# A decoder block on one core: triangular inverses from blocks of 32, their scratch on the weights' queue, and a diagonal by sums

## The chip, the cores and the metric

One core of a Trainium2 chip runs the whole program. The engines named below are TensorE (PE in the rows, its weight loads PEld), VectorE (DVE), ScalarE (ACT), GpSimd (POOL) and SyncE (SP, which here only issues transfers). The metric is the device time of one execution in microseconds. The matrices are float32; a large product is computed from two rounded parts (float32r) of each factor in three products.

## The reference, cut to what matters

One layer of a decoder on 256 positions of width 2048: a combined projection, three branches (gated delta rule with 8 heads, gated linear recurrence with 8 heads, attention into 256 memory tokens), their gated sum, an output projection and an MLP of width 8192. The change touches the first two branches:

```python
    lower = jnp.where(strict, bc[..., :, None] * jnp.einsum('bhnid,bhnjd->bhnij', kc, kc) * dec, 0.0)
    a_mat = lower + jnp.eye(CHUNK, dtype=lower.dtype)
    rhs = jnp.concatenate([vc * bc[..., None], kc * (bc * jnp.exp(gam))[..., None]], axis=-1)
    sol = lax.linalg.triangular_solve(a_mat, rhs, left_side=True, lower=True, unit_diagonal=True)
...
        dec = jnp.exp(jnp.where(causal[:, :, None], b_i[..., :, None, :] - b_i[..., None, :, :], -jnp.inf))
        a_i = jnp.einsum('bhtd,bhjd,bhtjd->bhtj', q_i, k_i, dec)
        o = (q_i * jnp.exp(b_i)) @ state + a_i @ v_i
...
    merged = ga * (oa @ w_br_a[l]) + gb * (ob @ w_br_b[l]) + gc * (oc @ w_br_c[l])
    x = x + rmsnorm(merged @ w_out[l], g_post_mix[l])
    m = jnp.square(jax.nn.relu(h2 @ w_mlp_in[l])) @ w_mlp_out[l]
```

The kernel takes chunks of 128 positions instead of 64, so it needs, for each of 8 heads and 2 chunks, the inverse of a unit triangular 128x128 matrix (the first excerpt), and for the second branch a 128x128 matrix `a_i` whose diagonal is a plain sum over the 128 features, since the decay there is 1.

## The kernel before, in words

The main stream is a row of units. A unit is 16 (or 8) tiles of 128 rows of a weight matrix by 512 columns; two tiles are a group: one load of 512 KB by SP into `w` (4 buffers), a rounded copy `wh` on ScalarE (line 174), the remainder `wl` on VectorE (line 175; 4 buffers of each), and products on TensorE, in `unit` 12 of 512 columns (lines 206 to 208), in `unit_joined` 8 of 512 and 8 of 256 columns (lines 225 and 227).

All other work is background: Python generators in a list `bg`. After a group, `tick` adds `rate[0]` to a credit and `pump` takes that many steps, a step being what a generator issues up to its next `yield`. Rates are set by stage: R1 while the first branch's q, k, v, z are projected (64 ticks), R2 in the attention branch (48), R3 in the second branch's projections (64), R4 in the gates of the first branch (48). The framework's scheduler may put an instruction ahead of earlier ones of its engine when its operands are there sooner; `pin` (`keep_in_program_order`) forbids it to stand ahead of the instruction of its engine that the code issues just before.

`gen_a`, once per group of four heads, is the delta rule: decays `dec`, Gram products `kk`, the triangular matrices `U` (8 per head group, transposed), then their inverses. VectorE solves the blocks of 16 on the diagonal: POOL copies these blocks to a DRAM scratch `scr` (8 transfers) and reads them back so that each partition holds its block's coefficients, `Lb` (8 transfers). In `for c in range(BL - 2, -1, -1)` (lines 885, 886) one product and one sum per column follow each other. Then rounds join pairs of blocks of 16, 32 and 64: products `pw` (line 916) and `pzt` (line 921) and eight transposes back into `X` (line 929), all on TensorE; the last round has narrow products of its own (lines 905 and 910). A plain float32 product is two instructions in the rows.

`gen_b` is the second branch. Its diagonal is computed by eight products of 128x128 per head group of which the identity mask keeps the diagonal alone (line 1064, tile `ad`). `gen_start` prepares constants beside the first units; its TensorE work is `rb`, `gcol`, `pc` and `pl`.

## Time and profile before

| | us |
|---|---|
| median of 3 runs (lowest, highest) | 1806.01 (1805.75, 1806.58) |
| profiled execution, its own time | 1806.44 |
| profiled execution, first to last instruction | 1804.7 |
| TensorE busy | 1793.5 |
| weight loads of TensorE busy | 1532.6 |
| VectorE busy | 1127.0 |
| ScalarE busy | 905.6 |
| GpSimd busy | 44.5 |

Busy time is the union of an engine's instructions over the span. Instructions of TensorE overlap in the records, so a group's mean duration is longer than the time that one more of them takes; what a piece takes is read from the chain of waits, where pieces follow each other in time.

### The profile page before, as it was taken

Reading aid. Unit: us, or ns where it says so; the run is one execution under the profiler, and the core shown is the slowest. Engines: PE = TensorE matmul, PEld = TensorE weight load, DVE = VectorE, ACT = ScalarE, POOL = GpSimd, SP = SyncE. Lnnn points to the kernel's source line nnn. Section 1 sums busy time; section 2 is a strip of 40 time slices with the busy share of each in tenths; the row PEclk is TensorE's granted clock in tenths of the full one; section 3 lists DMA queues with packets and bytes.
Section 4 is the critical chain, followed back from the end, with each engine's and each line's share of the span. In section 5 each row is a group of like instructions: output and inputs, shape, how many; then the busy total and the mean of one; then the engine's idle time right before and its main releaser. Section 6 shows DMA issues by size and latency. Waiting matters only on the chain.

```text
span 1804.7 us, 23851 instructions
## 1 busy us (share of the span) xinstructions
PE 1793.5 (99%) x9241; PEld 1532.6 (85%) x9241; DVE 1127.0 (62%) x1518; ACT 905.6 (50%) x1156; POOL 44.5 (2%) x68
## 2 busy tenths in 40 slices
PE   9999999999999999999999999999999999999998
PEld 7888888888888888888888888888888888888886
DVE  5865678755764677696555557655655565655556
ACT  6645565544555565555444445544444444444433
POOL 1000000200200000000000000000000000000000
PEclk9999999999999999999999999999999999999999
DMA  8665645754665556465666674666666676666664
GB/s 264 207 194 160 185 146 168 209 172 138 177 187 152 158 169 187 141 186 175 198 186 187 213 232 152 191 193 191 195 186 198 188 220 187 195 187 195 188 194 139
DMA packets 174946, 333.40 MB, mean 185 GB/s; under 512 B 13144, under 2 KB 14832, under 8 KB 174576
## 3 DMA queue, kind: packets, MB, share of 16 engines
q1 hardware_dynamic: 169280, 325.10, 58.7%
q10 hardware_dynamic: 4528, 4.54, 0.9%
q0 software_dynamic: 1024, 2.23, 0.7%
q8 instruction: 72, 1.18, 0.3%
q14 instruction: 42, 0.34, 0.1%
HBM read 329.60 MB, written 2.23 MB: 184 GB/s over the span
## 4 chain that ended last, share of the span: by engine, by line
PE 97%; DVE 1%; DMA 1%; ACT 1%; issue 0%; SPq 0%; DVEq 0%; POOLq 0%; POOL 0%; ACTq 0%
PE mm L225 23%; PE mm L206 18%; PE mm L207 18%; PE mm L208 18%; PE mm L227 12%; PE pa L1120 1%; DMA w<-in_w_kv_mem 0%; PE pzt L921 0%; PE pw L916 0%; PE mm L373 0%; PE mm L375 0%; PE mm L372 0%; DVE wl L175 0%; DMA w<-in_w_in 0%; DVE cv L718 0%
## 5 line engine op out<-in xcount | busy, mean ns | idle before, releaser
L175 DVE TENSOR_TENSOR wl<-w,wh 128x1024 fp32r<-128x1024 f32 x600 | 728.5, 1223 | 540.2 <-ACT wh L174 456.3
L174 ACT CAST wh<-w 128x1024 fp32r<-128x1024 f32 x600 | 628.0, 1052 | 719.0 <-PE mm L208 453.7
L206 PE MATMUL mm<-wh,hh 128*128 128x512 f32 x576 | 227.5, 395 | 0.3 <-DVE sum L266 0.3
L208 PE MATMUL mm<-wh,hh 128*128 128x512 f32 x576 | 224.7, 390 | 0.0
L225 PE MATMUL mm<-h2h,wh 128*128 128x512 f32 x960 | 224.4, 390 | 0.0
L207 PE MATMUL mm<-wl,hh 128*128 128x512 f32 x576 | 224.4, 390 | 0.0
L225 PEld LDWEIGHTS mm<-h2h,wh 128*128 128x128 f32 x960 | 178.3, 188 | 35.8
L206 PE MATMUL mm<-wh,mh 128*128 128x512 f32 x512 | 199.2, 389 | 0.0
L207 PE MATMUL mm<-wl,mh 128*128 128x512 f32 x512 | 199.2, 389 | 0.0
L208 PE MATMUL mm<-wh,ml 128*128 128x512 f32 x512 | 199.2, 389 | 0.0
L225 PE MATMUL mm<-hh,wh 128*128 128x512 f32 x768 | 184.8, 391 | 0.3 <-ACT z L730 0.3
L225 PEld LDWEIGHTS mm<-hh,wh 128*128 128x128 f32 x768 | 141.0, 188 | 27.8 <-ACT z L730 0.5
L208 PEld LDWEIGHTS mm<-wh,hh 128*128 128x128 f32 x576 | 108.1, 188 | 22.7
L206 PEld LDWEIGHTS mm<-wh,hh 128*128 128x128 f32 x576 | 108.2, 188 | 21.8 <-DVE sum L266 0.5
L207 PEld LDWEIGHTS mm<-wl,hh 128*128 128x128 f32 x576 | 108.3, 188 | 21.1
L227 PEld LDWEIGHTS mm<-h2h,wl 128*128 128x128 f32 x960 | 119.3, 192 | 2.3
L227 PE MATMUL mm<-h2h,wl 128*128 128x256 f32 x960 | 120.3, 283 | 0.0
L207 PEld LDWEIGHTS mm<-wl,mh 128*128 128x128 f32 x512 | 96.1, 188 | 20.0
L208 PEld LDWEIGHTS mm<-wh,ml 128*128 128x128 f32 x512 | 96.1, 188 | 19.9
L206 PEld LDWEIGHTS mm<-wh,mh 128*128 128x128 f32 x512 | 96.1, 188 | 19.9
L227 PE MATMUL mm<-hh,wl 128*128 128x256 f32 x768 | 102.2, 284 | 0.0
L227 PEld LDWEIGHTS mm<-hh,wl 128*128 128x128 f32 x768 | 98.9, 191 | 3.4
(388 smaller groups left out, 1913.9 us busy)
## 6 DMA issues: line engine op xcount, KB each, us to landing
w<-in_w_in SPq DMA_DIRECT2D x240, 512.0 KB, 4.0
w<-in_w_mlp_in SPq DMA_DIRECT2D x128, 512.0 KB, 4.0
w<-in_w_mlp_out SPq DMA_DIRECT2D x128, 512.0 KB, 4.2
w<-in_w_out SPq DMA_DIRECT2D x32, 512.0 KB, 4.1
w<-in_w_kv_mem SPq DMA_DIRECT2D x30, 512.0 KB, 4.9
w<-in_w_br_c SPq DMA_DIRECT2D x16, 512.0 KB, 4.1
w<-in_w_br_a SPq DMA_DIRECT2D x16, 512.0 KB, 4.5
w<-in_w_br_b SPq DMA_DIRECT2D x16, 512.0 KB, 3.6
```

Of the source, the lines that this page charges most:

```text
L174: q(A.copy(wh[:, js, 0:width], w[:, js, 0:width]))
L175: q(V.tensor_tensor(out=wl[:, js, 0:width], in0=w[:, js, 0:width], in1=wh.bitcast(F32)[:, js, 0:width], op=ALU.subtract))
L206: T.matmul(o, st, wh[:, j, :], start=kt == 0, stop=False)
L207: T.matmul(o, st, wl[:, j, :], start=False, stop=False)
L208: T.matmul(o, sl, wh[:, j, :], start=False, stop=kt == nk - 1)
L225: T.matmul(ps[c], wh[:, j, c * P:(c + 1) * P], both[j], start=k0 + j == 0, stop=end)
L227: T.matmul(ps[c][:, 0:S], wl[:, j, c * P:(c + 1) * P], both[j][:, 0:S], start=False, stop=end)
L1120: T.matmul(pas[h][:, t * 192:t * 192 + 192], kp[:, h, t * P:(t + 1) * P], qp[:, h * 2 + t, 0:192], start=True, stop=True)
```

## The change

Five things, beside new rates. (1) The blocks solved by substitution are of 32: of each pair of blocks of 16 the second is solved as before, then the coefficients between the two (`Lx`) are multiplied with it and summed, the first block's coefficients are read from the scratch, and a second substitution solves it. The joining round of width 16 is not run. (2) The scratch's transfers are issued by SP: 12 writes and 16 reads, then 4 reads between the two substitutions, per head group. (3) After the round of width 32 only the quarter of `X` that the last round reads is transposed back, in eight transposes of 64x64. (4) The diagonal in `gen_b` is the sum over partitions of k times q, by products with ones, in two rounded parts. (5) The first instruction of each background step on VectorE, ScalarE and TensorE is pinned. Beside these, `dec` gets a yield between VectorE's and TensorE's part, and the four TensorE pieces of `gen_start` stand in one step.

```diff
-R1, R2, R3, R4 = 1.1, 1.0, 1.0, 1.2
+R1, R2, R3, R4 = 1.1, 1.2, 1.2, 1.27
...
-    V, A, T, G = nc.vector, nc.scalar, nc.tensor, nc.gpsimd
+    G = nc.gpsimd
+    pin = tc.keep_in_program_order
+    class Placed:
+        def __init__(self, engine):
+            self.engine, self.step_begins = engine, False
+        def __getattr__(self, name):
+            op = getattr(self.engine, name)
+            def issue(*args, **kwargs):
+                ins = op(*args, **kwargs)
+                if self.step_begins:
+                    pin(ins)
+                    self.step_begins = False
+                return ins
+            return issue
+    V, A, T = Placed(nc.vector), Placed(nc.scalar), Placed(nc.tensor)
+    def step_marks(begins):
+        for e in (V, A, T):
+            e.step_begins = begins
...
         while n > 0 and bg:
+            step_marks(True)
             try:
                 next(bg[0])
                 n -= 1
             except StopIteration:
                 bg.pop(0)
+            step_marks(False)
...
+        rrs = []
+        for t in range(NT):
+            rrs.append(g4("rr", (P, P)))
+            V.tensor_scalar(out=rrs[t], in0=ones, scalar1=rsm[:, t:t + 1], scalar2=None, op0=ALU.mult)
+        yield
+        pt = bank("cols")
+        pg, pc, pl = pt[:, 256:288], pt[:, 288:384], pt[:, 384:392]
+        for t in range(NT):
+            T.matmul(pt[:, t * P:(t + 1) * P], rrs[t], ident, start=True, stop=True)
+        T.transpose(pg, grow, ident[0:32, 0:32])
+        T.transpose(pc, crow, ident[0:96, 0:96])
+        T.transpose(pl, lrow, ident[0:8, 0:8])
...
             dl = g4("dl", (P, 2, 4, P), F32R)
-            pd = bank("dec")
             for i, l_ in enumerate((ldh, ldl)):
                 V.tensor_tensor(out=dl[:, i], in0=bc(caus, 4),
                                 in1=l_.bitcast(F32)[:, t, hs].unsqueeze(2).to_broadcast([P, 4, P]), op=ALU.mult)
+            yield
+            pd = bank("dec")
+            for i in range(2):
                 T.matmul(pd, mgtr, dl[:, i].rearrange("p h i -> p (h i)"), start=i == 0, stop=i == 1)
...
+        scr = dp.tile([NB // 2, 3, 8, BL, BL], F32, tag="scr", name=nm("scr"))
+        Lx = [g4("Lx", (P, 4, BL * BL)) for t in range(NT)]
+        def spread(rows, src):
+            nc.sync.dma_start(rows, src.rearrange("k b c m -> k (b c m)").to_broadcast([rows.shape[0], rows.shape[1]]))
         for k in range(NB):
-            sl = slice(k * BL, (k + 1) * BL)
-            pin(G.dma_start(scr[k].rearrange("b c m -> c b m"), U[sl, :, sl]))
+            sl, w = slice(k * BL, (k + 1) * BL), k % 2 * 2
+            nc.sync.dma_start(scr[k // 2, w].rearrange("b c m -> c b m"), U[sl, :, sl])
         for k in range(NB):
-            G.dma_start(Lb[k * BL:(k + 1) * BL].rearrange("p b m -> p (b m)"),
-                        scr[k:k + 1].rearrange("k b c m -> k (b c m)").to_broadcast([BL, 8 * BL * BL]))
+            spread(Lb[k * BL:(k + 1) * BL].rearrange("p b m -> p (b m)"), scr[k // 2, k % 2 * 2:k % 2 * 2 + 1])
+        yield
+        for k in range(NB // 2):
+            r0 = 2 * k * BL
+            nc.sync.dma_start(scr[k, 1].rearrange("b c m -> c b m"), U[r0:r0 + BL, :, r0 + BL:r0 + 2 * BL])
+        for k in range(NB // 2):
+            r0 = 2 * k * BL
+            for t in range(NT):
+                spread(Lx[t][r0:r0 + 2 * BL].rearrange("p b m -> p (b m)"), scr[k, 1:2, t * 4:t * 4 + 4])
         yield
...
+        def substitute(w):
+            pin(V.memset(Lb[:, :, 0:BL * BL:BL + 1], 1.0))
+            for c in range(BL - 2, -1, -1):
+                n = BL - c
+                tm = lp.tile([P, 8, BL], F32, tag="tm", name=nm("tm"), bufs=2)
+                V.tensor_tensor(out=tm[:, :, 0:n], in0=Xc[:, :, w, c:BL], in1=Lb[:, :, c * BL + c:(c + 1) * BL],
+                                op=ALU.mult)
+                V.tensor_reduce(out=Xc[:, :, w, c], in_=tm[:, :, 0:n], axis=AX.X, op=ALU.add)
+                if c % 2 == 0:
+                    yield
+        yield from substitute(1)
+        for k in range(NB // 2):
+            spread(Lb[(2 * k + 1) * BL:(2 * k + 2) * BL].rearrange("p b m -> p (b m)"), scr[k, 0:1])
+        V.tensor_scalar(out=Xc[:, :, 0, :], in0=Xc[:, :, 1, :], scalar1=rsecond, scalar2=None, op0=ALU.mult)
+        for t in range(NT):
+            ts = slice(t * 4, t * 4 + 4)
+            lx = Lx[t].rearrange("p b (c m) -> p b c m", c=BL)
+            V.tensor_tensor(out=lx, in0=Xc[:, ts, 0, :].unsqueeze(2).to_broadcast([P, 4, BL, BL]), in1=lx, op=ALU.mult)
+            yield
+            V.tensor_reduce(out=Xc[:, ts, 0, :], in_=lx, axis=AX.X, op=ALU.add)
+            yield
+        yield from substitute(0)
+        V.scalar_tensor_tensor(out=Xc[:, :, 0, :], in0=Xc[:, :, 1, :], scalar=rfirst, in1=Xc[:, :, 0, :],
+                               op0=ALU.mult, op1=ALU.add)
...
-        for s in (s_ for s_ in (2, 4, 8, 16, 32, 64) if s_ >= BL):
+        for s in (s_ for s_ in (2, 4, 8, 16, 32, 64) if s_ >= 2 * BL):
...
+            if s == 32:
+                pt = bank("X")
+                for b in range(8):
+                    T.transpose(pt[0:64, b * 64:(b + 1) * 64], XT[0:64, b, 0:64], ident[0:64, 0:64])
+                A.copy(X[0:64, :, 0:64], pt[0:64, :].rearrange("p (b i) -> p b i", b=8))
+                yield
+                continue
...
         AT = g4("AT", (P, 8, P))
-        for t in range(NT):
-            pd = bank("ad")
-            for h in range(4):
-                T.matmul(pd[:, h * P:(h + 1) * P], k[:, h, t * P:(t + 1) * P], q[:, h, t * P:(t + 1) * P],
-                         start=True, stop=True)
-            V.tensor_tensor(out=AT.rearrange("p (h t) i -> p h t i", t=NT)[:, :, t, :],
-                            in0=pd.rearrange("p (h i) -> p h i", h=4), in1=bc(ident, 4), op=ALU.mult)
+        kq, kqh, kql = g4("kq"), g4("kqdh", dt=F32R), g4("kqdl", dt=F32R)
+        V.tensor_tensor(out=kq, in0=k.rearrange("p h s -> p (h s)"), in1=q.rearrange("p h s -> p (h s)"), op=ALU.mult)
+        yield
+        A.copy(kqh, kq)
+        V.tensor_tensor(out=kql, in0=kq, in1=kqh.bitcast(F32), op=ALU.subtract)
+        yield
+        for hp in range(2):
+            pd, cs = bank("ad"), slice(hp * 512, hp * 512 + 512)
+            T.matmul(pd, onesr, kqh[:, cs], start=True, stop=False)
+            T.matmul(pd, onesr, kql[:, cs], start=False, stop=True)
+            V.tensor_tensor(out=AT[:, hp * 4:hp * 4 + 4, :], in0=pd.rearrange("p (b i) -> p b i", b=4), in1=bc(ident, 4),
+                            op=ALU.mult)
         yield
```

## Rows read from the trace of the kernel before

**Rows 1.** The page: busy time of the engines and the share of the span, the granted clock in 40 slices, and the chain that ended last by engine.
```profile
PE 1793.5 (99%) x9241; PEld 1532.6 (85%) x9241; DVE 1127.0 (62%) x1518; ACT 905.6 (50%) x1156; POOL 44.5 (2%) x68
...
PEclk9999999999999999999999999999999999999999
...
PE 97%; DVE 1%; DMA 1%; ACT 1%; issue 0%; SPq 0%; DVEq 0%; POOLq 0%; POOL 0%; ACTq 0%
```

**Rows 2.** Who TensorE waited for: us in total, times, the longest. These are all its waits.
```profile
PE idle L336 <- POOL ident L84: 1.6, 1, 1.6
PE mm L373 <- DVE memT L277: 0.4, 1, 0.4
PE mm L225 <- ACT z L730: 0.3, 1, 0.3
PE mm L206 <- DVE sum L266: 0.3, 1, 0.3
```

**Rows 3.** The chain of waits from 385 to 424 us, where the first head group's blocks are joined: start, us, what.
```profile
389.14 1.73 PE pw L916 x16
390.87 0.29 PE mm L206
...
393.69 1.73 PE pzt L921 x16
...
398.22 0.87 PE X L929 x8
...
414.58 1.07 PE pw L905 x16
415.65 0.43 PE mm L206
```

**Rows 4.** The same view from 546 to 582 us, the second head group's round of width 16.
```profile
547.75 1.73 PE pw L916 x16
549.48 1.97 PE mm L227 x16
```

**Rows 5.** The same view from 630 to 640 us, the first head group's diagonal.
```profile
633.35 1.79 PE ad L1064 x16
```

**Rows 6.** The same view from 272 to 284 us, the first head group's dec products.
```profile
275.90 0.47 PE dec L798
...
276.60 0.31 PE dec L798
...
279.67 0.23 PE dec L798
```

**Rows 7.** Groups of instructions of VectorE and, in the second row, of ScalarE: line, operation, tiles and shapes, count, then busy us, mean ns of one, and idle time before them with what ended most of it. The last row is of another view, VectorE's busy time from 327 to 375 us in the instructions that write or read the tile xc.
```profile
L175 DVE TENSOR_TENSOR wl<-w,wh 128x1024 fp32r<-128x1024 f32 x600 | 728.5, 1223 | 540.2 <-ACT wh L174 456.3
L174 ACT CAST wh<-w 128x1024 fp32r<-128x1024 f32 x600 | 628.0, 1052 | 719.0 <-PE mm L208 453.7
...
L744 DVE TENSOR_REDUCE ss<-sq 128x8 f32<-128x1024 f32 x4 | 4.9, 1218 | 4.0 <-ACT sq L742 4.0
L796 DVE TENSOR_TENSOR dl<-caus,ldl 128x512 fp32r<-128x512 f32 x4 | 2.7, 684 | 0.0
L889 DVE TENSOR_TENSOR X<-xc,mblk 128x1024 f32<-128x1024 f32 x2 | 2.4, 1222 | 0.0
...
327.00:375.00 48.00, 7.76 (x31) 1.00 0.76 207
```

**Rows 8.** The chain of waits from 33 to 40 us, the constants' TensorE work.
```profile
36.13 0.44 PE rb L491 x4
...
36.81 0.17 PE gcol L106
...
37.21 0.15 PE pl L507
37.37 0.43 PE mm L207
```

**Rows 9.** Who ScalarE waited for, in total us, times and the longest: the rounded copies of weights for TensorE (units of 12 products), and for the landing of w_in's weights.
```profile
ACT wh L174 <- PE mm L208: 453.7, 289, 4.3
...
ACT wh L174 <- DMA w<-in_w_in: 11.3, 6, 2.7
```

**Rows 10.** Transfers: the queues (packets, MB, share of 16 engines' span), KB and us to landing of the weights' and the scratch's transfers, how long the weights' issue takes on SP (ns, least, median, most), and what POOL waited for before issuing the reads (us, times).
```profile
q1 hardware_dynamic: 169280, 325.10, 58.7%
...
q0 software_dynamic: 1024, 2.23, 0.7%
...
w<-in_w_in SPq DMA_DIRECT2D x240, 512.0 KB, 4.0
...
scr<-U POOLq DMA_DIRECT2D x16, 8.0 KB, 3.4
...
L163 SPq DMA_DIRECT2D w<-in_w_in x240: 367/368/639, 90.3 to 968.8; - x120
...
  DMA scr<-U: 1.9, 3
```

**Rows 11.** VectorE in two stretches: us, its busy time and instructions, granted clock, mean busy share of the 16 DMA engines, GB/s. The first has the first head group's scratch transfers, the second its substitution.
```profile
330.00:350.00 20.00, 13.41 (x21) 1.00 0.95 228
350.00:385.00 35.00, 25.15 (x48) 1.00 0.66 197
```

**Rows 12.** Groups of TensorE's instructions, by form: the wide products of the joins of width 16 and 32 in both head groups; busy us, mean ns of one.
```profile
L916 PE MATMUL pw<-X,U 128*128 128x64 f32 x64 | 7.6, 271 | 0.0
```

More of the change, by code (lines that the diff above doesn't have):

```diff
@@ L89, in tile_trunk @@
     x_r = a["x"][0].rearrange("(t p) n -> p t n", p=P)
-    pin = tc.keep_in_program_order
     def adma(out, in_):
@@ L418, in gen_masks @@
         pin(V.tensor_copy(mgtr, mgt))
+        pin(V.tensor_copy(onesr, ones))
         pin(V.tensor_copy(msk2[:, 0, :], mlt))
@@ L426, in gen_masks @@
             if b < P:
-                cur = mblk if b == BL else cst.tile([P, P], F32, tag=f"blk{b.bit_length() % 2}", name=f"blk{b}")
+                cur = cst.tile([P, P], F32, tag=f"blk{b.bit_length() % 2}", name=f"blk{b}")
                 v3 = cur.rearrange("p (n s) -> p n s", s=b)
@@ L438, in gen_masks @@
             pin(V.tensor_tensor(out=mT[s], in0=d, in1=mlt, op=ALU.mult))
+            if s == BL:
+                pin(V.tensor_tensor(out=mblk, in0=cur, in1=mT[s], op=ALU.subtract))
+                pin(V.tensor_reduce(out=rfirst, in_=mT[s], axis=AX.X, op=ALU.add))
+                pin(V.tensor_scalar(out=rfirst, in0=rfirst, scalar1=1.0 / BL, scalar2=None, op0=ALU.mult))
+                pin(V.tensor_scalar(out=rsecond, in0=rfirst, scalar1=-1.0, scalar2=1.0, op0=ALU.mult, op1=ALU.add))
             prev = cur
@@ L486, in gen_start @@
         yield
-        pb = bank("rb")
-        for t in range(NT):
-            rr = g4("rr", (P, P))
-            V.tensor_scalar(out=rr, in0=ones, scalar1=rsm[:, t:t + 1], scalar2=None, op0=ALU.mult)
-            T.matmul(pb[:, t * P:(t + 1) * P], rr, ident, start=True, stop=True)
-        V.tensor_copy(rbm, pb[:, 0:S])
-        yield
-        load_x()
-        turn_grow(grow, 32, 16)
-        yield
-        pc = bank("pc")
-        T.transpose(pc[:, 0:96], crow, ident[0:96, 0:96])
-        V.tensor_copy(ccol, pc[:, 0:96])
+        load_x()
+        yield
         for nm_, t in (("gn_a", gna), ("gn_b", gnb)):
@@ L505, in gen_start @@
         load_x()
-        pl = bank("pl")
-        T.transpose(pl[:, 0:8], lrow, ident[0:8, 0:8])
+        rrs = []
[10 more added lines that the diff above has]
+        T.transpose(pl, lrow, ident[0:8, 0:8])
+        V.tensor_copy(rbm, pt[:, 0:S])
+        V.tensor_copy(gcol[:, 16:48], pg)
+        V.tensor_copy(ccol, pc)
         raw, e, lb = small("raw", 8), small("e", 8), small("lb", 8)
@@ L877, in gen_a @@
         V.memset(W, 0.0)
-        V.memset(Lb[:, :, 0:BL * BL:BL + 1], 1.0)
-        Xc = lp.tile([P, 8, BL], F32, tag="xc", name=nm("xc"))
-        V.tensor_copy(Xc, dblk.unsqueeze(1).to_broadcast([P, 8, BL]))
+        Xc = lp.tile([P, 8, 2, BL], F32, tag="xc", name=nm("xc"))
+        V.tensor_copy(Xc[:, :, 1, :], dblk.unsqueeze(1).to_broadcast([P, 8, BL]))
         yield
-        for c in range(BL - 2, -1, -1):
-            n = BL - c
-            tm = lp.tile([P, 8, BL], F32, tag="tm", name=nm("tm"), bufs=2)
-            V.tensor_tensor(out=tm[:, :, 0:n], in0=Xc[:, :, c:BL], in1=Lb[:, :, c * BL + c:(c + 1) * BL], op=ALU.mult)
-            V.tensor_reduce(out=Xc[:, :, c], in_=tm[:, :, 0:n], axis=AX.X, op=ALU.add)
-            if c % 2 == 0:
-                yield
@@ new lines, in gen_a @@
+        yield from substitute(0)
+        V.scalar_tensor_tensor(out=Xc[:, :, 0, :], in0=Xc[:, :, 1, :], scalar=rfirst, in1=Xc[:, :, 0, :],
+                               op0=ALU.mult, op1=ALU.add)
+        V.tensor_tensor(out=X.rearrange("p b (k c) -> p b k c", c=2 * BL),
+                        in0=Xc.rearrange("p b w c -> p b (w c)").unsqueeze(2).to_broadcast([P, 8, NB // 2, 2 * BL]),
+                        in1=mblk.rearrange("p (k c) -> p k c", c=2 * BL).unsqueeze(1).to_broadcast([P, 8, NB // 2, 2 * BL]),
+                        op=ALU.mult)
@@ L1060, in gen_b @@
         AT = g4("AT", (P, 8, P))
[L1061 to L1067 removed]
+        kq, kqh, kql = g4("kq"), g4("kqdh", dt=F32R), g4("kqdl", dt=F32R)
[9 more added lines that the diff above has]
+            V.tensor_tensor(out=AT[:, hp * 4:hp * 4 + 4, :], in0=pd.rearrange("p (b i) -> p b i", b=4), in1=bc(ident, 4),
+                            op=ALU.mult)
         yield
```

7 lines of the change are left out of this document (2 added, 5 removed).

## The prediction

> **What bounds the kernel now.** I read the page first. TensorE is busy 99% of the span at a granted clock of 9 tenths or more in every slice (mean 0.999, the 2.4 GHz level throughout), and the chain of work that ended last lies on TensorE for 97% [rows 1]. The reader is to see that no other engine is near: VectorE 62%, ScalarE 50%. Busy is not yet bound, so the next view is who waits: TensorE waited 2.6 us in all, 1.6 of it at the very start [rows 2]. Then the chain in short stretches, because there the pieces follow one another without gaps and so give what each piece really takes: a 512-column product takes 0.23 us [rows 6], a 256-column one 1.97 / 16 = 0.12 [rows 4]. A background step (a block of other TensorE work between two weight groups) appears as one piece, and the product after it is a little longer. So the time is the sum of TensorE's pieces, and the question is which pieces the change takes out, and whether anything makes TensorE wait.
>
> That reading has a critic. The Trainium skill, page "Perfetto Trace Analysis", section "Identifying the Most-Contended Engine", says matmul occupancy is a bad measure of how near TensorE is to its limit and that the busy share of weight loads should be used. Here that share is 85% [rows 1], which by the rule leaves 15% of headroom; the pieces that follow each other without a gap do not agree. It is a rival below.
>
> **Taken out on TensorE.** Per head group (there are two):
> - The join round of width 16 goes. In the first group it is 1.73 (pw x16) + 1.73 (pzt x16) + 0.87 (X x8), and the product behind pw takes 0.29 instead of 0.23 [rows 3], which I take behind pzt too: 4.45 us. In the second group pw is 1.73 again [rows 4]; counted the same. Two groups: -8.9 us.
> - In the round of width 32 the eight transposes back (like the 0.87 of [rows 3]) become eight of 64x64. The nearest row is the 64x64 products: 16 in 1.07, and 0.20 more on the product behind [rows 3], so eight cost 0.54 + 0.20 = 0.74. Bounds: 0.74 to the old 0.87. I take 0.74: -0.3 us for both.
> - The diagonal of AT: sixteen pieces, 1.79 us [rows 5], become four 512-column products, 4 x 0.23 = 0.92. Two groups: -1.7 us. Its cover is gone if the operand (product, rounding, remainder, one step each) is late; the nearest row of a late operand is dec, where a product takes 0.47 instead of 0.23 [rows 6]. Bound: +0.24 per step, 0.5 in all.
> - The four dec products stand in the same step as the VectorE work they need and cost 0.47 + 0.31 + 0.23 + 0.23 = 1.24 (the fourth like the third) [rows 6]. With a yield between them they should cost 0.92: -0.6 us. Bounds 0 to -0.6; I take -0.6, since one step later is a whole weight group (12 x 0.23 = 2.7 us) and two of the VectorE products take 1.4 [rows 7].
> - At the start rb, gcol, pc and pl run as two blocks, with 0.43 on the product behind the second [rows 8]. As one block they save one such break: -0.2 us, bounds 0 and -0.4.
>
> Sum: -8.9 - 0.3 - 1.7 - 0.6 - 0.2 = -11.7 us.
>
> **Added on VectorE.** The second substitution repeats 30 small instructions: the 31 instructions on xc before the joins take 7.76 us, of which X takes 1.22 [rows 7], so 6.5. The two products over Lx and the two sums are 1024 wide, 1.22 each by the nearest rows [rows 7]: 4.9. A memset and two small ones of 6.5 / 30 = 0.22 each: 0.7. kq and its remainder add 2 x 1.22. Together 14.5 us per group, 29 us on an engine with 1804.7 - 1127.0 = 678 us idle: costed at nothing. What hides it: ScalarE waits for TensorE to give back the split-weight buffers (453.7 us in the units of 12 products alone [rows 9]), so the splits run ahead as far as four buffers allow. Three groups of 2.7 us less one rounding (1.05) and one remainder (1.22) [rows 7] leave about 5.9 us in which VectorE may be late. In the substitution itself (22 steps at 1.2 steps per group: 18.3 groups, 50 us) VectorE has 13.1 + 4.9 + 0.7 + 1.2 (X) = 19.9 us of steps and 18.3 x 1.22 = 22.3 of splits, 84%: it holds, with little to spare for evacuations. ScalarE loses four copies per group and gains two: nothing.
>
> **Moved to SP.** Per group POOL issued 8 writes and 8 reads; SP now issues 12 writes, 16 reads and later 4 more, at 0.37 us each by the weights' own row [rows 10]: 12 us in three bursts. SP is in order, so every weight load (one per 2.7 us) stands behind them, and the reads wait for the writes' landing (3.4 us median; POOL stood 1.9 us for it in all [rows 10]). The bytes: queue 0 took 0.7% of 16 engines' span for 2.23 MB, i.e. 202 us of engine time, 91 us per MB, against 52 for the weights [rows 10]. The first burst grows from 1.05 MB to 2.1 MB of reads: 2.1 x 91 / 16 = 12 us of all sixteen engines, 6.8 at the weights' rate. Against that, a weight load may be late by: four buffers x 2.7 = 10.9 between one split and the next in the same buffer, less 2.3 for the split, less 4.0 landing [rows 10] = 4.6 us until ScalarE waits, plus the 5.9 above = 10.5 until TensorE waits. In the old burst the engines were 95% busy [rows 11], ScalarE waited for weights 11.3 us over the whole w_in [rows 9], and TensorE not once [rows 2]. New lateness: between 0 (loads slip in between, as nothing pins the order) and 12 + 3.4 + 12 x 0.37 = 19.8 us. The two ends of the cost are 0 and 9.3 us per group. I take 0.3 per group, the near end: old lateness was absorbed with all of the 5.9 left, and twice that is still about the slack.
>
> The Trainium skill, page "DMA: Bandwidth & Descriptors", section "Queues, rings and completion order", says each engine consumes one ring's descriptors in order and takes turns between rings, which speaks against this move: before, weights took turns with the scratch, now they stand behind it. Its section "Issuing engines are not separate DMA queues" says the issuing engine only changes issue time. By the first the cost leans to the far end, by the second it is the extra bytes alone. No row here shows which holds for a burst on the weights' own queue.
>
> **Kept in place, and the rates.** A pin lets a step's first instruction start no earlier than its predecessor in the code. On TensorE there is little that runs early: gcol, pc and pl stand in one block though the code yields between them [rows 8]. What early or late steps cost TensorE is about 1 us (0.4 + 0.3 + 0.3 of waits after the start [rows 2], and the long dec pieces), part of it counted above. So the pins are costed at nothing, bounds -0.5 to +1. Steps: each group gains 2 (dec) + 1 (scratch) + 12 (sums, second substitution) - 3 (round) = 12, and gen_b 2, 28 in all; the rates give 48 x 0.2 + 64 x 0.2 + 48 x 0.07 = 25.8 more. So the background ends about where it did, two steps over; those stand beside the next unit, 22 us long.
>
> **The sum.** -11.7 + 0.6 (SP) = -11.1 on the profiled execution's span of 1804.7, 1806.44 in its own time; the median is 1806.01, 0.4 lower, and taking the change from it gives 1794.9 us.
>
> **The rivals.**
> - Weights partly late behind the scratch: 3 us per group, a third of the far end, 1806.0 - 11.7 + 6 = 1800.3. For: the engines' 95% and a queue in order. Against: 10.5 us of slack and no wait in the old burst.
> - VectorE cannot keep up in the substitution: 16% more work than reckoned, from evacuations and a late transfer back, fills the 50 us; 8 us more than that, less the slack of 5.9, is a wait of some 2 us per group, 1806.0 - 11.7 + 4 = 1798.3. For: the 84%. Against: in the old substitution VectorE was busy 25.15 of 35 us [rows 11] and TensorE did not wait.
> - Slower: every scratch transfer of a burst is issued ahead of the next weight load in both groups and served in order: 19.8 us late, 9.3 waited, twice: 1806.0 - 11.7 + 18.6 = 1812.9. It turns to slower where a load is late by more than 16.4 us (10.5 + 5.9) in each group.
> - TensorE is not the bound, something else fills the freed pieces: 1806. Against: its pieces leave no gap. For it stands only the 85%.
> - More than the sum: the pins also end the small waits after early steps and the dec and start pieces save their utmost, 1793.0.
>
> **How the numbers follow.** Forecast 0.71 (its own range 1793.3 to 1797.5), weights partly late 0.12, VectorE 0.06, slower 0.04, TensorE not the bound 0.02, more than the sum 0.05. What a measurement can tell from no change is about 0.2%, 3.6 us: faster is below 1802.4. The forecast, VectorE, more, and all but 0.02 of weights partly late are faster: 0.92. The 0.02 and the not-bound case are the same: 0.04. Slower 0.04. Range 1792.5 to 1801: outside it lie the slower and unbound cases, the upper end of the late weights and little below.
>
> **What would show it.** Right: the wide products of the joins (now 64 instructions at L916 [rows 12] and as many at L921) halve to 32 each, AT comes as four pieces of 0.23 us per group, the last TensorE piece ends some 11 us earlier and TensorE's waits stay under 4 us in all. Wrong: a wait of TensorE on DMA or on VectorE's wl near 330 or 500 us, ScalarE's wait for weights well above 11.3 us with pieces of 512 columns over 0.23 behind it, or products behind the steps that got longer everywhere.

## The result: slower, 1811.6 us

The changed kernel takes 1811.58 us (median of 12 runs, 1809.17 to 1815.41) beside 1806.55 for the kernel before in the same rounds (12 runs, 1805.75 to 1806.82): a ratio of 1.003, interval 1.0021 to 1.0039. The forecast was 1794.9. The profiled execution is the fastest of the 12 (1809.17 in its own time, span 1807.5), so what its trace shows of the loss is the least of it. Of the runs below, only the profiled one of e1, at a granted clock of 0.65 throughout, is left out of the numbers.

From the page of the changed kernel: busy times, to be laid beside [rows 1]. Its instructions on VectorE, ScalarE and TensorE all carry line 56 (the wrapper that pins), so they are read by their tiles.

```profile
PE 1787.8 (99%) x9137; PEld 1521.5 (84%) x9137; DVE 1153.0 (64%) x1599; ACT 904.6 (50%) x1150; POOL 25.5 (1%) x36
```

The page's chain gives TensorE 79% here, but its shares add up to 86% only, so they are not to be laid beside the 97% of [rows 1]; e10 below, which lost almost nothing, has 82%. The waits say more. Who TensorE waited for in the changed kernel (us in total, times, the longest), beside [rows 2]; below it a row of who ScalarE waited for, beside [rows 9]:

```profile
PE mm L56 <- ACT wh L56: 4.4, 3, 2.3
PE mm L56 <- DVE wl L56: 3.2, 6, 0.8
PE idle L56 <- POOL ident L109: 1.6, 1, 1.6
...
ACT wh L56 <- DMA w<-in_w_in: 22.5, 13, 5.3
```

TensorE waits 11.1 us in all instead of 2.6, nearly all of it more for the two parts of weights, and ScalarE waits twice as long for w_in's landing. The pieces that were to become shorter did. The changed kernel's chain of waits from 395 to 470 us, where the first head group's blocks are joined, beside [rows 3]:

```profile
425.62 1.73 PE pw L56 x16
...
430.17 1.73 PE pzt L56 x16
...
434.73 0.56 PE X L56 x8
...
438.23 1.07 PE pw L56 x16
```

One wide round instead of two, and the eight small transposes in 0.56 (0.87 before, [rows 3]). To sum this over the span I took for every background block the time from the product before it to the product behind it, less two usual products (0.227 each, 0.1196 for 256 columns): 117.8 us over all blocks before, 107.2 now, 10.6 less. The same sum over the main stream alone, its time beyond the usual products, is 3.9 us before and 17.3 now. Less 10.6 and plus 13.4 is the span's 2.8 more. The 13.4 stand in three places: 1.6 in the first 50 us, 7.6 at 330 to 365 us (by estimate 1.7 of them at TensorE's lower clock, see the last section), 3.5 at 505 to 570, and 0.7 elsewhere. The stretches of the scratch transfers, by windows (us, then busy time and count of PE, PEld, DVE, ACT, POOL, granted clock, DMA share, GB/s), first of the kernel before and then of the changed one:

```profile
330.00:365.00 35.00, 35.00 (x166) 29.28 (x165) 24.71 (x46) 19.66 (x33) 5.81 (x12) 1.00 0.82 213
505.00:570.00 65.00, 65.00 (x393) 57.81 (x392) 39.78 (x63) 34.62 (x42) 0.00 (x0) 1.00 0.56 166
```

```profile
330.00:365.00 35.00, 30.20 (x126) 23.59 (x125) 21.10 (x35) 15.05 (x20) 2.04 (x1) 0.95 0.82 210
505.00:570.00 65.00, 62.62 (x342) 53.86 (x342) 45.10 (x81) 36.35 (x52) 0.00 (x0) 1.00 0.77 202
```

What SP issued in the first of them, in the changed kernel (start us, us, what):

```profile
318.70 6.57 SPq L188 DMA_DIRECT2D w<-in_w_in  x3
330.93 3.65 SPq L893 DMA_DIRECT2D scr<-U  x8
334.63 3.66 SPq L889 DMA_DIRECT2D lb<-scr  x8
338.33 3.89 SPq L899 DMA_DIRECT2D scr<-U  x4
343.09 0.39 SPq L188 DMA_DIRECT2D w<-in_w_in  x1
344.97 3.56 SPq L889 DMA_DIRECT2D Lx<-scr  x8
348.63 11.29 SPq L188 DMA_DIRECT2D w<-in_w_in  x8
```

After 325.3 us SP stands 5.7 us for the last of U (the coefficients that the scratch takes) and then issues 28 scratch transfers at 0.46 each (3.65 / 8), with the waits for their landing between; one weight load goes out in 23 us, where TensorE takes one group per 2.7. ScalarE then waits 5.31 us for a landing and TensorE 2.31 for the cast.

### The profile page after: what moved, and what is told of

The parts are those of the page before. It is cut to its first block, busy times and chain, and to the rows that moved or that the text cites. A ratio compares the mean times of both kernels' runs of the same rounds, so it can differ in the third digit from the quotient of the medians.

```text
span 1807.5 us, 23730 instructions
## 1 busy us (share of the span) xinstructions
PE 1787.8 (99%) x9137; PEld 1521.5 (84%) x9137; DVE 1153.0 (64%) x1599; ACT 904.6 (50%) x1150; POOL 25.5 (1%) x36
## 4 chain that ended last, share of the span: by engine, by line
PE 79%; DVE 3%; DMA 1%; ACT 1%; issue 1%; SPq 1%; POOL 0%; DVEq 0%; POOLq 0%; ACTq 0%
PE mm L56 75%; PE pa L56 1%; DVE wl L56 1%; DMA w<-in_w_in 1%; SPq L889 0%; PE kk L56 0%; DMA scr<-U 0%; PE pw L56 0%; PE pzt L56 0%; PE o L56 0%; ACT wh L56 0%; PE tr L56 0%; PE y L56 0%; PE mgT L56 0%; POOL r L327 0%
## 5 line engine op out<-in xcount | busy, mean ns | idle before, releaser
L56 DVE TENSOR_TENSOR wl<-w,wh 128x1024 fp32r<-128x1024 f32 (+1 forms) x610 | 738.8, 1220 | 531.4 <-ACT wh L56 458.1
L56 ACT CAST wh<-w 128x1024 fp32r<-128x1024 f32 (+1 forms) x610 | 636.8, 1050 | 731.9 <-PE mm L56 620.7
L56 PE MATMUL mm<-wh,hh 128*128 128x512 f32 x1152 | 367.1, 393 | 3.5 <-ACT wh L56 3.2
L56 PE MATMUL mm<-wh,oh 128*128 128x512 f32 x128 | 50.2, 392 | 0.0
L56 PE MATMUL mm<-wh,mgh 128*128 128x512 f32 x128 | 50.0, 390 | 0.0
```

What stands on the lines that cost most here:

```text
L56: ins = op(*args, **kwargs)
```

## Experiments

Each time is a median with its lowest and highest run, the ratio is to the kernel before on the same chip with its interval.

**Queue, pins, bytes.** e1 puts all scratch transfers of the changed kernel on POOL; e4 the writes alone; e2 puts before's own 32 transfers on SP; e3 leaves out the pins of the steps.

e1, the read and the two writes (in e4 the writes alone):

```diff
-            nc.sync.dma_start(rows, src.rearrange("k b c m -> k (b c m)").to_broadcast([rows.shape[0], rows.shape[1]]))
+            G.dma_start(rows, src.rearrange("k b c m -> k (b c m)").to_broadcast([rows.shape[0], rows.shape[1]]))
...
-            nc.sync.dma_start(scr[k // 2, w].rearrange("b c m -> c b m"), U[sl, :, sl])
+            pin(G.dma_start(scr[k // 2, w].rearrange("b c m -> c b m"), U[sl, :, sl]))
```

e2, in the kernel before:

```diff
-            pin(G.dma_start(scr[k].rearrange("b c m -> c b m"), U[sl, :, sl]))
+            nc.sync.dma_start(scr[k].rearrange("b c m -> c b m"), U[sl, :, sl])
...
-            G.dma_start(Lb[k * BL:(k + 1) * BL].rearrange("p b m -> p (b m)"),
+            nc.sync.dma_start(Lb[k * BL:(k + 1) * BL].rearrange("p b m -> p (b m)"),
```

e3:

```diff
-            step_marks(True)
...
-            step_marks(False)
```

> The changed kernel with all scratch transfers issued by POOL again (its writes pinned as in the kernel before), nothing else undone. Theory A (weight loads stand behind the scratch in SP's order): in the trace of after, SP issues one weight load between 325.3 and 348.6 us, TensorE loses 7.6 us at 330 to 365 us and 3.5 us at 505 to 570 us; both should go, time 1796 to 1799 us (before less the 10.7 us that the background pieces lost, plus some 2 us at the start). Theory B (the pins hold VectorE's and ScalarE's steps and with them the splits): unchanged, 1809 to 1813. Theory C (the larger volume of reads or VectorE's second substitution): unchanged or nearly so, over 1806.

> The kernel before with one part of the change alone: its 8 writes and 8 reads per head group issued by SP, unpinned. Theory A: 16 issues of 0.47 us and a wait for U and for the landing make a weight load 8 to 15 us late against a slack of about 10, so 0 to 5 us per group: 1807 to 1814, most likely 1809. Theories B and C: 1806.5, nothing in it that they blame.

> The changed kernel without the pins on the steps' first instructions, scratch still on SP. Theory A: still over 1808, the stretches at 330 to 365 and 505 to 570 us lose as much as in after within 3 us. Theory B: 1796 to 1799.

> The changed kernel with the scratch's writes issued by POOL and its reads still by SP. It parts theory A in two: if the harm is SP's wait for U and the writes' issue (16.6 us from the wait to the last write of the first group), the time falls to 1797 to 1800; if it is the reads' issue and their wait for the landing, it stays over 1805.

e1: 1809.15 (1805.81 to 1812.41), 1.0015 (1.0006 to 1.0024). Off SP's queue the change is still 12 us above 1797, so the queue alone is not the loss. e2: 1814.0 (1813.4 to 1814.29), 1.0043 (1.003 to 1.0055): yet the same move costs the kernel before 8 us. e3: 1812.56 (1811.63 to 1813.31), 1.0035 (1.0022 to 1.0047): the pins are not the cause. e4: 1811.83 (1810.94 to 1812.67), 1.0031 (1.0019 to 1.0043): no gain. None of these runs varies the new rates of the background; no run does.

e5 is the kernel of e1 once more, for its trace. e6 is before with its scratch read two times more into tiles that nobody uses. e7 is before with part (4) and the yield of `dec` alone, both as in the diff of the change. e6:

```diff
+        Lx = [g4("Lx", (P, 4, BL * BL)) for t in range(NT)]
+        for k in range(NB):
+            for t in range(NT):
+                G.dma_start(Lx[t][k * BL:(k + 1) * BL].rearrange("p b m -> p (b m)"),
+                            scr[k:k + 1, t * 4:t * 4 + 4].rearrange("k b c m -> k (b c m)").to_broadcast([BL, 4 * BL * BL]))
```

> The changed kernel with all its scratch transfers on POOL's queue (writes pinned), once more, for a profile at full clock: e1_pool came out at 1809.2, some 12 us above the 1797 that theory A (only the place of the transfers on SP's queue) gives. What is to be read is where those 12 us stand. Theory A in its weaker form: nothing is left at 330 to 365 and 505 to 570 us (under 1 us beyond the nominal rate there), and the rest is in the first 50 us. Theory C (the burst of scratch bytes, twice that of before, delays the weight loads on the DMA engines, whichever queue issues them): 4 us or more beyond the nominal rate stand at 330 to 365 and at 505 to 570 us together, with ScalarE or VectorE waiting for a weight load whose issue was in time and whose landing was late. Rival D (the clock): TensorE falls to the half clock in one or more stretches of 3.4 us, at some 1.7 us each.

> The kernel before, its queues untouched, with each of its scratch reads on POOL made two times more into a tile that nobody reads (16 reads of 64 KB more in each of the two groups, some 2.1 MB in all more than before). Theory C (the bytes of the burst alone delay the weights): slower by 4 to 12 us, 1810 to 1818, with ScalarE's wait for weights up by as much at 330 to 380 and 510 to 560 us. Theory A (only where they are issued): within 1 us of before, 1805 to 1807.

> The kernel before with two parts of the change alone: the diagonal products made by sums in place of the second set of TensorE products, and the yield after the fourth of the decay broadcasts; the substitution, the scratch and the queues as before. Theory of the sum: -1.7 for the diagonal and -0.6 for the yield, so 1803.7, between 1803.2 and 1804.5. Rival (what TensorE saves here is given back, because something else sets the pace of the recurrent part): 1805.5 to 1806.5.

e5: 1809.89 (1806.07 to 1812.0), 1.0016 (1.0005 to 1.0026). Its loss stands where the changed kernel's does: 4.7 us beyond the usual products at 330 to 365 and 6.7 at 505 to 570. At the first place SP no longer stands still, yet ScalarE waits for weights (first two rows), and the four loads issued from 338 to 347 us take 9.9 to 12.6 us to land (third row; fourth row: e10 below, where VectorE frees the buffers more evenly and TensorE loses nothing; 5.1 to 8.4 in the kernel before). So late weight loads are there without SP's queue too, as theory C had it, if not from the bytes alone (e15 below).

```profile
343.65 1.05 ACT L56 CAST wh<-w 128x1024 fp32r<-128x1024 f32 x1 [5.92 <-DMA w<-in_w_in]
351.11 1.04 ACT L56 CAST wh<-w 128x1024 fp32r<-128x1024 f32 x1 [5.45 <-DMA w<-in_w_in]
...
DMA to landing us min/median/max: 9.9/11.2/12.6
...
DMA to landing us min/median/max: 5.8/8.5/8.7
```

VectorE of e5 at the second place (start us, us, what, idle before and what ended it), and TensorE's wait:

```profile
519.10 0.17 DVE L56 MEMSET lb<- 128x128 f32 x1 [6.79 <-DMA scr<-U]
...
520.47 1.21 DVE L56 TENSOR_TENSOR mg<-mm,sg 128x1024 f32<-128x1024 f32 x1
...
521.74 3.78 PE L56 MATMUL mm<-hh,wh 128*128 128x512 f32 x8 [3.91 <-DVE mg L56]
```

The substitution's first instruction stands at VectorE's head for 6.8 us until its coefficients have landed (the row names a write of U that lands at the same moment; the last of the coefficients lands 0.3 us earlier), and behind it stands the gate product that TensorE needs. e6: 1831.49 (1830.81 to 1832.73), 1.014 (1.0123 to 1.0157), far above theory C's 1818, with the same picture in the first group (what VectorE and TensorE waited for):

```profile
DVE lb L883 <- DMA Lx<-scr: 11.1, 1, 11.1
...
PE mm L206 <- DVE sum L266: 11.8, 2, 11.6
PE mm L225 <- ACT sg L1009: 8.8, 1, 8.8
```

The 8.8 us stand in the second group, for the gate's activation `sg`, which ScalarE runs there behind three copies that wait for weights. So a late landing need not go through the weights: it holds up whatever the scheduler put behind the first reader. e6 did not separate bytes from that, since the reads also made the scheduler choose another order.

e7: 1805.57 (1804.77 to 1806.28), 0.9995 (0.9986 to 1.0005): 0.9 us under the 1806.48 of the same rounds, where the sum said 2.3; the interval just takes in both. Its diagonal pieces are the short ones (0.92 and 0.95 instead of 1.79 each), but steps later in the group moved, and its trace has a new wait that takes that back (who TensorE waited for):

```profile
PE oT L766 <- DVE on L757: 1.8, 1, 1.8
```

**The burst, the start and the yield.** e8 is e1 with the second batch of transfers (4 writes, the reads into `Lx`) three steps into the first substitution; e11 the same on SP; e9 is e8 with the start as before; e10 is e9 without the yield in `dec`.

e8, from e1 (the moved lines are the 4 writes and 8 reads):

```diff
-        for k in range(NB // 2):
-            r0 = 2 * k * BL
...
-        yield from substitute(1)
+        sub = substitute(1)
+        for i in range(3):
+            next(sub)
+            yield
+        for k in range(NB // 2):
+            r0 = 2 * k * BL
...
+        yield from sub
```

e9, from e8, and behind it e10, from e9:

```diff
-        pt = bank("cols")
...
+        pb = bank("rb")
...
+        turn_grow(grow, 32, 16)
...
+        pc = bank("pc")
```

```diff
                                 in1=l_.bitcast(F32)[:, t, hs].unsqueeze(2).to_broadcast([P, 4, P]), op=ALU.mult)
-            yield
             pd = bank("dec")
```

> The changed kernel with its scratch transfers on POOL's queue, and with the second batch (4 writes and the 8 reads into Lx) issued three steps into the first substitution instead of right behind the first batch; nothing else moved. Theory E (the burst: twice the broadcast bytes at once make this group's blocks and the weight loads land late; e5 showed VectorE waiting 6.8 us for the first substitution's blocks with TensorE 3.9 us idle behind it at 521 us, and weights landing late at 343 and 351): VectorE's wait for the blocks goes, and most of the 11.4 us beyond the nominal rate that e5 had at 330 to 365 and 505 to 570 us with it: 1800 to 1804. Rival F (the step that the decay's yield added lets VectorE do two pieces' work in one stretch, 11 us without a weight remainder at 324 to 335 us, whatever the scratch does): 330 to 365 us keeps its 4 to 5 us, and the time stays at 1805 to 1809.

> As e8_pool_late, and the start stage as it was before the change (its small transposes at their old steps). If the start's merged block is what puts 1.6 to 1.9 us more than before into the first 50 us, the time is 1 to 2 us under e8's; if those belong to the landing of the first weights and x whatever the block does, it is within 0.5 us of e8's or 0.2 to 0.4 above it.

> As e9_pool_late_start, without the yield between the decay's masks and its products. Rival F: VectorE's 11 us without a weight remainder at 324 to 335 us breaks up as in the kernel before (remainders at 328 and 333), the waits at 330 to 365 us go, and the time is 3 to 5 us under e9's although the yield's own 0.6 us are given up. Theory E: 0.3 to 0.8 us above e9's.

> As e8_pool_late, but with all scratch transfers on SP's queue as in the changed kernel: beside the changed kernel, e1 and e8 it makes a square of queue and burst. If the queue costs by itself (theory A in part), it stands 2 to 6 us above e8's; if the burst is all that costs, within 1 us of e8's.

e8: 1809.12 (1804.12 to 1810.89), 1.0013 (1.0003 to 1.0022). e9: 1805.12 (1803.13 to 1807.37), 0.9996 (0.9987 to 1.0005). e10: 1799.16 (1798.44 to 1799.95), 0.9962 (0.9947 to 0.9976), the first version below the kernel before. e11: 1803.58 (1802.62 to 1804.75), 0.9986 (0.9977 to 0.9996), 5.5 us *under* its twin on POOL, which no theory had. e8 keeps 4.6 us at 330 to 365, as rival F said, and misses theory E's 1800 to 1804. In e10 the two stretches are nearly full again:

```profile
330.00:365.00 35.00, 35.00 (x165) 29.26 (x164) 25.05 (x44) 19.79 (x35) 13.09 (x27) 1.00 0.94 240
505.00:570.00 65.00, 64.37 (x352) 55.81 (x350) 52.13 (x99) 34.46 (x40) 5.86 (x12) 1.00 0.74 216
```

What the yield does is read from VectorE's weight remainders: in the changed kernel (first fence) none starts between 323.65 and 334.78, because two pieces' `jk`, `U` and `AQ` work and the convolution follow each other; in e10 (second) they alternate (one more at 324.79), and so free the weight buffers: each load of the stretch goes out about 1.2 us after the start of a remainder.

```profile
323.65 1.22 DVE L56 TENSOR_TENSOR wl<-w,wh 128x1024 fp32r<-128x1024 f32 x1
334.78 1.22 DVE L56 TENSOR_TENSOR wl<-w,wh 128x1024 fp32r<-128x1024 f32 x1
```

```profile
329.55 1.23 DVE L56 TENSOR_TENSOR wl<-w,wh 128x1024 fp32r<-128x1024 f32 x1 [0.86 <-ACT wh L56]
334.05 1.21 DVE L56 TENSOR_TENSOR wl<-w,wh 128x1024 fp32r<-128x1024 f32 x1
```

The start: two rows of TensorE in the changed kernel.

```profile
36.13 0.50 PE L56 MATMUL mm<-wl,memT 128*128 128x512 f32 x1 [0.46 <-DVE wl L56]
40.26 0.50 PE L56 MATMUL mm<-wl,memT 128*128 128x512 f32 x1 [0.77 <-DVE wl L56]
```

Three loads of x stand among the weights there, as they do before. Before, the pieces `rb`, `gcol`, `pc` and `pl` filled TensorE at 36.1 to 37.4 us [rows 8]; with them moved behind 45 us TensorE comes to those weights before their remainders are ready. As pieces the block saves nothing: 1.21 us before, 1.20 as one. In e8's trace the waits there (0.5, 1.3 and 0.8) are followed by a fall of TensorE's clock at 42.1 us, in e16's, below, they are not.

**Undoing the parts in the changed kernel.** e12 takes the yield of `dec` alone out of it, e13 the yield and the start's block; e14 is e10 on SP's queue.

The edits of e12 and e13 are those of e10 and e9; e14 is, for all scratch transfers of e10:

```diff
-            G.dma_start(rows, src.rearrange("k b c m -> k (b c m)").to_broadcast([rows.shape[0], rows.shape[1]]))
+            nc.sync.dma_start(rows, src.rearrange("k b c m -> k (b c m)").to_broadcast([rows.shape[0], rows.shape[1]]))
```

> The changed kernel without the yield between the decay's masks and its products; all else as it is. Theory G (the yield's extra step and the burst together: VectorE frees its weight buffers 5 to 7 us late just when the scratch transfers hold up the loads; e9 to e10 gave 6.0 us): 1804.5 to 1807. Theory A (SP's queue alone makes the gap between the loads): the 23 us with one weight load stay, and the time is 1810 to 1812.5.

> As e12_after_no_yield, and the start stage as before the change. By e8 and e9 the start's merged block costs 1.5 to 4 us: 1.5 to 4 us under e12. What is then left over the sum of the prediction (1794.9, less 0.8 for the two parts undone, so 1795.7) is the price of the scratch transfers where the change puts them: with theory A 6 us or more is left (1802 or more), with theory G under 5.

> As e13, with the second batch of transfers (4 writes, 8 reads into Lx) three steps into the first substitution. The sum less the parts undone is 1795.7; if the late batch lets the loads keep pace on SP too, 1796 to 1799 and under e10 (1799.2, the same on POOL) or beside it; if SP's order still holds loads up, 1800 to 1803.

e12: 1820.03 (1817.56 to 1824.91), 1.0083 (1.0064 to 1.0102). e13: 1816.06 (1812.88 to 1820.89), 1.0057 (1.0039 to 1.0074). e14: 1810.67 (1808.13 to 1811.68), 1.0023 (1.0014 to 1.0032). The yield that cost 6 us on POOL saves 8 on SP; neither theory had that. e14 lies above every number of its expectation. VectorE of e12 has remainders at 331.55 and 333.29, much as e10 does (329.55 and 334.05), but SP is inside the scratch by then:

```profile
329.85 3.65 SPq L892 DMA_DIRECT2D scr<-U  x8
...
342.15 0.39 SPq L188 DMA_DIRECT2D w<-in_w_in  x1
344.15 3.56 SPq L888 DMA_DIRECT2D Lx<-scr  x8
347.82 14.12 SPq L188 DMA_DIRECT2D w<-in_w_in  x7
```

In the changed kernel, with the yield, the remainder that starts at 334.78 is the first to free a buffer after 324.9, so for ten microseconds from 325.3 SP, standing for U and issuing the first writes, holds up nothing that could have gone out. That is how I read the two signs; it was not tried by itself.

**Burst and start once more, in the best surrounding.** e15 is e10 with both batches at once on POOL, e16 is e10 with the change's start.

e15 undoes the edit of e8 in e10, e16 that of e9:

```diff
-        sub = substitute(1)
...
+        yield from substitute(1)
```

```diff
-        pb = bank("rb")
...
+        pt = bank("cols")
```

> e10 with the second batch of scratch transfers (4 writes, 8 reads into Lx) right behind the first, on POOL's queue. Theory E (the burst of bytes delays blocks and weights): 3 to 10 us over e10, 1802 to 1809, with VectorE waiting for the first substitution's blocks at some 515 us or weights landing late. Theory A (only SP's queue costs): within 1 us of e10's 1799.2.

> e10 with the change's start stage (its small transposes in one block). If that block moves TensorE against the first weights' and x's landing as e8 and e9 say, 1.5 to 4 us over e10: 1800.7 to 1803.2, all of it in the first 50 us; if what it showed there belongs to the yield's or the queue's surrounding, within 0.5 us of e10 or 0.2 under it.

e15: 1808.7 (1807.92 to 1811.22), 1.0017 (1.0007 to 1.0026). e16: 1802.42 (1800.17 to 1803.48), 0.9978 (0.9969 to 0.9988). The start's block has now three pairs, and costs 4.0 (e8 to e9), 4.0 (e12 to e13, four runs each, whose ranges overlap) and 3.3 us (e10 to e16). The runs of e16 lie in two clumps, three at 1800.2 to 1800.6 and seven at 1802.1 to 1803.5; the profiled one, of the first, has no fall of the clock in the start. Part of the block's price is thus probably the lower clock after its waits.

e15 looks like theory E, but its trace speaks against it: TensorE loses nothing at 330 to 365 us, though the four loads issued there from 335 to 344 us take 6.4 to 9.6 us to land, and POOL issues the reads into `Lx` at nearly the same times as in e10 (347.4 and 507.2 beside 346.3 and 505.2 us), wherever the code has them. What differs is the order on VectorE and on ScalarE. First e15, then e10, both around the second group:

```profile
507.24 3.92 POOL L886 DMA_DIRECT2D Lx<-scr  x8 [4.21 <-DMA scr<-U]
...
511.56 0.17 DVE L56 MEMSET lb<- 128x128 f32 x1
...
512.58 1.02 ACT L56 ACTIVATE sg<-mm 128x1024 f32<-128x1024 f32 x1
513.66 3.48 PE L56 MATMUL mm<-hh,wh 128*128 128x512 f32 x8 [4.50 <-ACT sg L56]
...
516.97 0.25 DVE L56 TENSOR_REDUCE xc<-tm 128x8 f32<-128x96 f32 x1
...
518.21 1.16 DVE L56 TENSOR_TENSOR mg<-mm,sg 128x1024 f32<-128x1024 f32 x1
519.43 2.11 PE L56 MATMUL mm<-hh,wh 128*128 128x512 f32 x8 [1.14 <-DVE mg L56]
```

```profile
496.88 1.02 ACT L56 ACTIVATE sg<-mm 128x1024 f32<-128x1024 f32 x1
...
505.19 3.94 POOL L886 DMA_DIRECT2D Lx<-scr  x8 [3.41 <-ACT wh L56]
...
506.78 1.23 DVE L56 TENSOR_TENSOR mg<-mm,sg 128x1024 f32<-128x1024 f32 x1 [0.41 <-PE mm L56]
...
518.48 0.17 DVE L56 MEMSET lb<- 128x128 f32 x1
```

TensorE's long wait of 4.5 us is for the gate's activation `sg`, which ScalarE runs at 512.58 in e15, behind rounded copies and `off` products, and already at 496.88 in e10. The wait of 1.1 us behind it is VectorE's: the scheduler put eleven columns of the substitution, in one piece from 511.56 to 517.2, ahead of the gate product `mg`. So I asked whether the order is the cause.

**The order held.** e17 (the changed kernel) and e18 (e15) keep all instructions of the three engines in the program's order, from the scratch to the end of the second substitution.

```diff
-                if self.step_begins:
+                if self.step_begins or held[0]:
...
+        held[0] = True

         def spread(rows, src):
...
         yield from substitute(0)
+        held[0] = False
```

> The changed kernel, with every instruction of VectorE, ScalarE and TensorE that is issued between the scratch and the end of the second substitution of a group kept in the program's order, so that weight remainders alternate with the background's steps. Theory H (the order is the cause): the waits at 330 to 365 and 505 to 570 us, 11.4 us together, fall to under 5 and the time to 1803 to 1806. Theory A (SP's queue holds up the loads whatever the order): the gap between the loads at 325 to 348 us stays, and the time is 1809 to 1814.

> e15 with the order held in the same way. Theory H: most of the 9.5 us between e15 and e10 comes back, 1799 to 1803. Theory E (the burst of bytes): the time stays at 1807 to 1810. If the program's order is itself a poor one (ScalarE or VectorE waiting at the head for blocks of the scratch), it is above 1810, and the trace names the instruction that stands at the head.

e17: 1859.81 (1854.7 to 1861.84), 1.0293 (1.0277 to 1.0309). e18: 1859.27 (1858.93 to 1860.11), 1.0295 (1.0278 to 1.0312). The program's order is a poor one, the last case of e18's expectation; theory H's numbers do not come, but the order that it blames was replaced by a worse one, so it is not tested. What ScalarE waited for in e18 from 300 to 620 us:

```profile
ACT wh L58 <- PE mm L58: 63.2, 36, 3.6
ACT sum L58 <- PE mm L58: 34.4, 7, 8.7
ACT off L58 <- PE kk L58: 31.6, 4, 12.0
```

The `off` products stand at ScalarE's head up to 12 us for `kk`, with the weights' casts behind them. What the pair does show is the size of the lever: in e18 the transfers of e15 are unchanged, and order alone moves the time by 50 us, the lower clock after the new waits included (0.988 on average, 0.998 in e15).

## Why the prediction was wrong, point by point

- **Taken out on TensorE, -11.7: right, -10.6 in this trace.** The wide round went, X is 0.76 with the lengthening of the product behind it (0.74 taken, 0.88 before in the same measure), the diagonal 0.93 a group (0.92 taken), `dec` 0.93 (0.92 taken).
- **The start, -0.2: wrong in sign.** It costs 3.3 to 4.0 us in three pairs of medians, 1.6 in the changed kernel's fastest run. The step that failed is the one that counted only the break behind a block; the pieces stood at 36 us in front of weights whose remainders were not ready, and the prediction did not ask what TensorE would meet there without it.
- **Moved to SP, "I take 0.3 per group, the near end": the main miss.** The step that failed is this term, lateness absorbed by 10.5 us of slack. The two stretches hold 11.1 us more than before, 7.6 and 3.5, instead of 0.6. For SP's queue, the ground, that loads slip in between, does not hold in the trace: one load in 23 us. The issue term was too small as well, 0.46 each instead of 0.37, and SP's wait for the last of U (5.7 us) was not in the 19.8. But the queue is not the whole of it: on POOL (e5) the same stretches hold 4.7 and 6.7. There VectorE frees no weight buffer for 11 us, the loads that follow land late, and in the second group the substitution's first instruction stands ahead of the gate product. The slack of four buffers supposed that VectorE frees them in time. The far end was 9.3 a group, and its rival's 1812.9 lies 1.3 us from the measured 1811.6; but that is partly chance, since a fifth to a quarter of the miss is the start's and the second group lost only 3.5.
- **The Trainium skill's rule** (page "DMA: Bandwidth & Descriptors", section "Queues, rings and completion order": one ring in order, turns between rings). The weight loads on SP did stand behind the scratch, as SP's rows show, but there already in the issuing queue, at transfers not yet issued. Its other section, "Issuing engines are not separate DMA queues", by which another issuing engine saves only the time of issuing, does not cover this either: the issuing engine changed the time by 11.5 us in one surrounding (e10 to e14) and by 5.5 the other way in another (e8 to e11), if with other orders of instructions.
- **VectorE at nothing: half right.** It has 26 us more (29 taken), and it is not full. But what costs is which instruction stands at its head: e5 and e6, and e15 for 1.1 us, show TensorE waiting behind substitution work. ScalarE, put at nothing as well, holds up TensorE in the same way through `sg`: 4.5 us in e15, 8.8 in e6. The prediction weighed both by how much work they have, not by its order.
- **The steps: wrong.** The yield in `dec`, taken at -0.6, is worth -8 us in one surrounding and +6 in another, by the order that it leads to.
- **Pins at nothing: right within 1 us** (e3).
- **TensorE not the bound: right to reject.** Where nothing is late, TensorE is busy for the whole of a stretch again (e10 at 330 to 365 us).

Of the 16.7 us between forecast and median, 3.3 to 4.0 are the start's by the three pairs. In the profiled execution the miss is 14.3, of which 13.4 are waits of the main stream and what follows them; the 2.4 from there to the median go with a lower mean clock (0.998 in the profiled execution, 0.997 on average). Beside the start, the loss stands where the scratch and the substitution are: through late weight loads, behind SP's queue in the changed kernel's own trace and late in landing on POOL, and through the order on VectorE and ScalarE, seen on POOL. That the two stretches hold it is shown; how much each would cost alone stays open, because every move of a transfer also made the scheduler choose another order, and the attempt to hold the order (e17, e18) replaced it by a worse one. The new rates were tried in no run by themselves, and the second substitution was never taken out alone. e10, which keeps both, is 1799.2, within 3.5 us of the sum less the two parts undone (1795.7).

## What to carry to other kernels

Before a transfer that waits for computed data goes on the queue that also feeds the main stream, look at what is queued behind it: in the changed kernel that waited too, for the data (5.7 us), for 28 issues (0.46 each) and for the landings. Here the move cost 8 us (e2) and 11.5 (e10 to e14), but gained 5.5 in another surrounding (e8 to e11), so try it. When a block of work is taken from a place, look at what it was covering there. And where a scheduler orders the instructions, a saving of 10 us can vanish in the new order of an engine that is far from full: look at what stands at the head of each queue, and try the parts of a change one by one on top of the best version.

## What the runs showed of the hardware that was not expected

After short waits TensorE's granted clock fell to its lower level, half of the higher. In the changed kernel TensorE waited four times between 347 and 355.5 us, 0.8 to 2.3 us each, and from 355.25 the clock was 0.50 for 3.41 us; the waits of 0.5 and 0.8 us in its start brought no fall. Windows of the changed kernel, before and in the fall:

```profile
352.00:355.20 3.20, 0.50 (x1) 0.19 (x1) 0.94 (x1) 1.68 (x2) 0.00 (x0) 1.00 1.06 388
355.30:358.60 3.30, 3.06 (x7) 2.48 (x8) 2.94 (x4) 2.41 (x3) 0.00 (x0) 0.50 0.90 287
```

Seven products take 3.06 us in the second window, about twice their usual 0.227 each, so by estimate this fall costs 1.7 us on top of the waits: more than half of the 2.8 us by which the profiled span is longer. The kernel before has none before the work's end, and neither has e10; the changed kernel has one in its profile, and e8 three, one of them in the start stage (42 us). The changed kernel's runs lie 6 us apart where those of before lie within 1.1, and their mean clocks go from 0.998 for the fastest to 0.995 for the slowest, beside 0.999 in the profile of before. By estimate that difference of clock, 0.003 of 1810 us, is 5 us, nearly all of the spread; and a mean of 0.997 beside 0.999 makes some 3.6 of the 5.0 us between the two medians. So a short wait can cost more than its own length: the products after it are slower too.

Moving 32 small transfers with not a byte more to the weights' queue cost the kernel before 8 us (e2). On POOL the weight loads issued during the scratch's reads took 9.9 to 12.6 us to land in e5, where the median over w_in is some 4.
